# A bidirectional mLSTM and convolution layer on one core: its sweeps with whole fp32 products of the states, in an order laid down by a list schedule

## The chip, the cores and the metric

The kernel runs on one core of a Trainium2 chip. The metric is the device time of one execution in microseconds, smaller is better; times of several runs are given by their median.

## What is computed

One layer works on two sequences, a prompt of 1024 rows and a sample of 256 rows, each row 1024 numbers wide. They are handled as one sequence of 1280 rows, that is ten chunks of 128 rows (chunks 0 to 7 the prompt, 8 and 9 the sample). The reference, cut to what matters here:

```python
h = rms_norm(x, norm_g) * (1.0 + scale) + shift
cb, cc, cx, cz, q, k, v, o, mz, gpre, gmerge = split_combined(h @ w_in)
y_conv = cb * centred_dwconv3(cc * cx, conv_w, conv_b) * jax.nn.silu(cz)
# mlstm_chunkwise, one direction, per head (4 heads of 256), per chunk of 128 rows:
S   = einsum('td,sd->ts', qc, kc) * Dexp
num = einsum('ts,sd->td', S, vc) + inter_w * einsum('td,de->te', qc, C)
hm  = num / den
C   = decay * C + einsum('s,sd,se->de', w, kc, vc)        # the state, 256 x 256
# forward and backward results are added, normalised per head, and gated:
y_m = jax.nn.sigmoid(o) * hm * jax.nn.silu(mz)
merged = g_conv * (y_conv @ w_proj_conv) + g_mlstm * (y_m @ w_proj_mlstm)
out = rms_norm(x + gate * (merged @ w_out))
```

The state C passes from chunk to chunk, forward in one sweep and backward in the other. A chunk needs its incoming states of both directions before it can be finished. All results are float32.

## The kernel before

**Two ways to multiply.** Most products are made of split operands: a float32 tensor becomes a high part (a rounded copy of type fp32r, made on ScalarE) and a low part (the rest, made on GpSimd or VectorE), and TensorE adds three fp32r products, high by high, high by low and low by high. A product of operands of type float32 without a split is one instruction in the code; the trace shows it as two matmul records.

**The stages.** First come the modulation and the norm. Then `run` (L471) works through a list of products of the input projection (seven for each pair of column blocks, a Strassen scheme): one `product` (L330) is 24 matmuls of 320 columns, and beside it run the splits of the next weights and the work on earlier results. Generators can be stepped once per product: `weights` (L852) prepares exponentials, and `thirds` (L819) forms the gate row on VectorE out of eight blocks `wg`, each in two loads; per block it ends in a small matmul with `ones` (L823). Results that later stages need (q, k, v, the convolution branch `yc_dr`, the gates `og_dr` and `th_dr`) go to DRAM. k is stored twice: transposed in `kT_dr`, and by rows, already split, as `kn_drH` and `kn_drL`.

Up to L1054 (`hand.close()`) the instructions of each engine stand in the order in which the program calls them. From there on the framework's own scheduler orders them.

**The sweeps** (L1161 to L1379) go over four heads. `backward(h)` runs one sweep ahead and keeps its queries in `qcb`; `forward(h)` then finishes the chunks in pairs, while `backward(h + 1)` runs beside it. In a sweep, per chunk:

- `prep` (L1122) loads the two parts of k, weights v with `w` on ScalarE (`vH`) and forms the low part on VectorE (`vL`, L1129).
- `state` (L1143) makes 2 x 3 fp32r products of 258 columns into `pu` (L1150 to L1152), adds them to the decayed state C on VectorE (L1157; L1155 for a first chunk), and splits C with `split` (L1103): the high part on ScalarE (L1106), the low part on GpSimd (L1107).
- `query` (L1133) splits q in the same way, multiplies 2 x 3 times with the parts of C into `pq` (L1140), and copies the result out, scaled, on ScalarE (L1141).

`chunk_pair` (L1176) makes the scores q times k (L1192, plain float32), weighs them (L1196), forms the divisors `r` (L1199 to L1202), transposes the weighted scores (L1213), multiplies them with v (L1220, plain float32), and adds the two queries. `mlstm_out` (L1266) normalises five, three or two chunks together, transposes (L1282), gates with `og` (L1283), and stores `ym_dr`.

**The filler.** `zc_units` (L1317) is the product of the convolution branch with its projection: 32 units of 24 matmuls of 320 columns (L1312 to L1314), independent of the sweeps. Its inputs `y` come from `yc_dr` in two halves of the rows. `FILL` and `BACK` (L1344, L1345) say after which step of a sweep a unit is called.

**The end.** `merge` (L1395) multiplies one half of `ym_dr` with its projection (384 matmuls of 320 columns, into `accd`), and `finish` (L1408) makes the output projection (480 matmuls of 256 columns, L1422 to L1424), the residual and the last norm. The first half of the rows goes first.

All DMAs are issued from SyncE (SP in the profile), in one queue whose entries wait in turn.

Of the kernel before, what the change touches and what calls it, by code (L numbers as in the profile page):

```python
# [9 lines left out]
F32 = mybir.dt.float32  # L10
# [6 lines left out]
P = 128  # L17
# [22 lines left out]

@with_exitstack
def encoder_kernel(
# [35 lines left out]
    kn_dr = [dram.tile([T, D], F32, name="kn_dr" + part) for part in "HL"]  # L78
# [91 lines left out]
    def quarter(pool, nm):  # L170
        return tuple(pool.tile([P, 4, TH2], F32R, name=nm + part) for part in "HL")
# [152 lines left out]

    hstack = ctx.enter_context(ExitStack())
    hp = hstack.enter_context(tc.tile_pool(name="hp", bufs=1, side="right"))
    B = {(0, 0): quarter(hp, "b00"), (1, 0): quarter(hp, "b10"), (1, 1): quarter(hp, "b11")}


# [289 lines left out]
    def turn_one(p):  # L619
# [9 lines left out]
        def f():  # L629
            vt = [qtile() for _ in range(1 + key)]  # L630
            for (j0, jn), pv in zip(((0, 3), (3, 2)), pvs):
                js = slice(j0 * P, (j0 + jn) * P)
                if key:
                    A.copy(vt[0][:, js].bitcast(F32R), pv[:, :jn * P])
                    V.tensor_tensor(out=vt[1][:, js].bitcast(F32R), in0=pv[:, :jn * P], in1=vt[0][:, js],
                                    op=ALU.subtract)
                else:
                    A.copy(vt[0][:, js], pv[:, :jn * P])
            for dst, o in zip(kn_dr if key else (v_dr,), vt):
                store(dst[l * TH2:(l + 1) * TH2, r0:r0 + P].rearrange("(c p) d -> p c d", p=P),  # L640
                      o[:].rearrange("p (c d) -> p c d", d=P))
# [177 lines left out]
    def thirds(pool):  # L819

        def total(acc, n):
            pg = misc_tile()
            PE.matmul(pg[0:1, 0:2 * P], ones[:, 0:1], acc[:].rearrange("p s n -> p (s n)"), start=True, stop=True)  # L823
            yield
            V.tensor_scalar(out=acc[0:1].rearrange("p s n -> p (s n)"), in0=pg[0:1, 0:2 * P], scalar1=0.5, scalar2=None,
                            op0=ALU.mult)
            for s in range(2):
                store(gb_dr[s:s + 1, n * P:(n + 1) * P], acc[0:1, s])

        late = iter(())  # L830
        for n in range(KT):
            ns = slice(2 * D + n * P, 2 * D + (n + 1) * P)
            acc = pool.tile([P, 2, P], F32, tag="acc", bufs=2, name="gacc")
            G.memset(acc[:], 0.0)
            for s in range(2):
                dma(acc[0:1, s], b_ada[0:1, ns])
            for k in range(0, KT, 4):
                raw = pool.tile([P, 4, P], F32, tag="wg", bufs=1, name="wg")
                dma(raw[:], wada[:, k:k + 4, ns])
                next(late, None)  # L840
                yield
                next(late, None)
                yield
                for i in range(4):
                    for s in range(2):
                        V.scalar_tensor_tensor(out=acc[:, s], in0=raw[:, i], scalar=cols[:, 8 * s + k + i:8 * s + k + i + 1],
                                               in1=acc[:, s], op0=ALU.mult, op1=ALU.add)
            late = chain([None], total(acc, n))
        for _ in late:
            yield  # L850
# [196 lines left out]
    with tc.tile_pool(name="r2", bufs=5, side="right") as ring[0], \  # L1047
            tc.tile_pool(name="ab", bufs=1, side="right") as conv_pool[0]:
        run(ends[9])
        settle()  # L1050
    with tc.tile_pool(name="r4", bufs=8, side="right") as ring[0]:
        run(len(todo))
        settle()
    hand.close()  # L1054

# [7 lines left out]
    misc[0] = bstack.enter_context(tc.tile_pool(name="psB", bufs=3, space=PSUM))  # L1063
    psM = bstack.enter_context(tc.tile_pool(name="psM", bufs=1, space=PSUM))

    def acc_tile():
        return psM.tile([P, 512], F32, tag="acc", bufs=2, name="acc")

    yp = ctx.enter_context(tc.tile_pool(name="yp", bufs=8, side="right"))
# [3 lines left out]
    qcbs = [qkv.tile([P, NC - 2, HD + 2], F32, name=f"qcb{i}") for i in range(2)]  # L1073
    Cbuf = [qkv.tile([P, 2, HD + 2], F32, name=f"C{d}") for d in range(2)]
# [10 lines left out]
    def slot(c):  # L1085
        return c - (c > 7)

    def load_head(h, what):
        i, hs = h % 2, slice(h * HD, (h + 1) * HD)
        for t0, tn in ((640, 384), (0, 640), (1024, 256)):  # L1090
            ts_ = slice(t0, t0 + tn)
            cs = slice(t0 // P, (t0 + tn) // P)
            if "k" in what:
                dma(kTs[i][:, :, ts_], kT_dr[hs, ts_].rearrange("(b p) t -> p b t", p=P))
            if "v" in what:
                dma(vNs[i][:, cs, 0:HD], v_dr[ts_, hs].rearrange("(c p) d -> p c d", p=P))
            if "q" in what:
                dma(qTs[i][:, :, ts_], qT_dr[hs, ts_].rearrange("(b p) t -> p b t", p=P))
# [434 lines left out]
```

## Time and profile before

| | us |
|---|---|
| median of 3 runs (1824.59 to 1827.71) | 1827.34 |
| the profiled execution | 1823.46 |
| its span | 1821.7 |
| TensorE busy in it (93%) | 1693.2 |
| VectorE, ScalarE, GpSimd busy | 1030.8, 667.6, 831.4 |
| end of the input projection, last matmul of L337 | about 1232.8 |
| first matmul of `merge` | 1582.3 |
| last matmul | 1812.3 |

The span is what the trace covers; the profiled execution's time is 1.8 us longer. A matmul's busy time runs to the modelled end of its pipeline, 0.28 to 0.32 us, while the next one starts 0.12 to 0.15 us after it; so what a matmul costs in a dense row is the distance between two starts. "idle before" is the time in which an engine did nothing before an instruction, with what ended it. The prediction shows the lines that it rests on.

### The profile page before, as it was taken

How to read it: one execution, taken by the hardware profiler on the slowest of the kernel's cores; microseconds unless marked ns; L12 is line 12 of the kernel's file. 1: busy time of each engine (PE TensorE's matmuls, PEld its weight loads, DVE VectorE, ACT ScalarE, POOL GpSimd, SP SyncE). 2: the span in 40 equal slices, each digit the busy share in tenths (PEclk: the TensorE clock that was granted, in tenths of full speed). 3: DMA queues.
4: the chain of work that ended last, by engine and by line, in shares of the span. 5: the costliest groups of instructions: out<-in, count | busy, mean ns of one | idle time of the engine just before them, and what ended most of it. 6: DMA issues, size and time to landing. Idle time of an engine off the chain costs nothing.

```text
span 1821.7 us, 30022 instructions
## 1 busy us (share of the span) xinstructions
PE 1693.2 (93%) x11438; PEld 1630.9 (90%) x11438; DVE 1030.8 (57%) x1739; ACT 667.6 (37%) x1359; POOL 831.4 (46%) x661
## 2 busy tenths in 40 slices
PE   5789999999899999999999999996888788899997
PEld 1689999999788999999999999996877678799997
DVE  6874333277987554555555333332588777456645
ACT  6552333223434222222222223122576565434323
POOL 3443333234545466666665433333566364232422
PEclk9889999999999999999999999998999999999999
DMA  8223234223655222222221534349767865674631
GB/s 308 63 87 108 98 104 133 84 85 92 168 146 145 62 64 76 76 76 72 68 69 46 167 96 145 121 135 318 256 205 225 282 184 163 217 244 152 225 128 70
DMA packets 231427, 253.28 MB, mean 139 GB/s; under 512 B 13700, under 2 KB 190068, under 8 KB 230260
## 3 DMA queue, kind: packets, MB, share of 16 engines
q1 hardware_dynamic: 231284, 251.37, 43.7%
q8 instruction: 90, 1.47, 0.3%
q14 instruction: 53, 0.43, 0.1%
HBM read 177.85 MB, written 73.47 MB: 138 GB/s over the span
## 4 chain that ended last, share of the span: by engine, by line
PE 54%; DVE 6%; POOL 3%; issue 2%; DMA 2%; ACT 2%; SPq 0%; DVEq 0%; POOLq 0%; ACTq 0%
PE accx L337 35%; PE accd L1312 2%; PE accd L1313 2%; PE accd L1314 2%; PE accd L1423 2%; PE accd L1424 2%; PE accd L1422 2%; PE pq L1140 1%; POOL C1L L1107 1%; PE acc L1313 1%; PE acc L1312 1%; PE acc L1314 1%; POOL wl L161 1%; POOL C0L L1107 1%; PE misc L627 1%
## 5 line engine op out<-in xcount | busy, mean ns | idle before, releaser
L409 DVE TENSOR_TENSOR q<-accx,q 128x640 f32<-128x640 f32 x288 | 233.3, 820 | 420.2 <-PE accx L337 368.0
L161 POOL TENSOR_TENSOR wl<-comb,wh 128x512 fp32r<-128x512 f32 x176 | 236.3, 1344 | 488.3 <-ACT wh L160 403.3
L161 POOL TENSOR_TENSOR wl<-raw,wh 128x512 fp32r<-128x512 f32 x196 | 270.8, 1386 | 194.2 <-ACT wh L160 179.1
L337 PE MATMUL accx<-half,wh 128*128 128x320 f32 x1408 | 268.2, 313 | 5.4 <-ACT wh L160 5.4
L160 ACT CAST wh<-comb 128x512 fp32r<-128x512 f32 x176 | 108.6, 620 | 388.7 <-DVE comb L379 305.7
L337 PEld LDWEIGHTS accx<-half,wh 128*128 128x128 f32 x1408 | 223.5, 190 | 6.8 <-ACT wh L160 5.6
L160 ACT CAST wh<-raw 128x512 fp32r<-128x512 f32 (+1 forms) x212 | 136.2, 648 | 92.5 <-PE accd L1313 27.9
L337 PE MATMUL accx<-half,wl 128*128 128x320 f32 x704 | 162.2, 312 | 0.8 <-POOL wl L161 0.8
L498 ACT ACTIVATE q<-q,zero 128x640 f32<-128x640 f32 x80 | 66.4, 830 | 174.4 <-DVE q L409 155.3
L337 PEld LDWEIGHTS accx<-half,wl 128*128 128x128 f32 x704 | 119.0, 190 | 1.5 <-POOL wl L161 1.5
L1423 PE MATMUL accd<-wl,mH 128*128 128x256 f32 x320 | 90.2, 282 | 0.1
L1422 PE MATMUL accd<-wh,mH 128*128 128x256 f32 x320 | 90.1, 282 | 0.0
L1424 PE MATMUL accd<-wh,mL 128*128 128x256 f32 x320 | 90.0, 282 | 0.0
L337 PE MATMUL accx<-b10H,wh 128*128 128x320 f32 x352 | 82.4, 315 | 6.1 <-ACT q L934 5.9
L337 PE MATMUL accx<-t2H,wl 128*128 128x320 f32 x352 | 81.9, 314 | 4.2 <-POOL wl L161 4.1
L337 PE MATMUL accx<-b00H,wh 128*128 128x320 f32 x352 | 81.8, 314 | 2.4 <-DVE half L248 2.3
L337 PE MATMUL accx<-t2H,wh 128*128 128x320 f32 x352 | 82.4, 316 | 1.8 <-ACT wh L160 1.7
L1312 PE MATMUL acc<-y,wh 128*128 128x320 f32 x256 | 81.8, 323 | 0.7 <-ACT wh L160 0.3
L1313 PE MATMUL acc<-y,wh 128*128 128x320 f32 x256 | 81.2, 317 | 1.1 <-DMA y<-yc_drL 1.1
L337 PE MATMUL accx<-t3H,wh 128*128 128x320 f32 x352 | 80.6, 310 | 1.1 <-ACT wh L160 1.1
L1312 PE MATMUL accd<-y,wh 128*128 128x320 f32 x256 | 78.1, 313 | 3.5 <-DVE og L1283 3.5
L337 PE MATMUL accx<-b10H,wl 128*128 128x320 f32 x352 | 81.1, 312 | 0.2 <-POOL wl L161 0.2
(304 smaller groups left out, 4539.5 us busy)
## 6 DMA issues: line engine op xcount, KB each, us to landing
raw<-in_w_in_dram SPq DMA_DIRECT2D x96, 256.0 KB
raw<-in_w_in_dram SPq DMA_DIRECT2D x44, 512.0 KB
th_dr<-q SPq DMA_DIRECT2D x32, 320.0 KB
th<-th_dr SPq DMA_DIRECT2D x32, 320.0 KB
wa<-in_w_ada_dram SPq DMA_DIRECT2D x8, 1024.0 KB
raw<-in_w_proj_conv_dram SPq DMA_DIRECT2D x16, 512.0 KB
kH<-kn_drH SPq DMA_DIRECT2D x64, 128.0 KB
kL<-kn_drL SPq DMA_DIRECT2D x64, 128.0 KB
```

The costliest lines, as they stand in the source:

```text
L160: A.copy(wh[:], src)
L161: eng.tensor_tensor(out=wl[:], in0=src, in1=fp(wh[:]), op=ALU.subtract)
L337: PE.matmul(acc[:, q, 0:TQ], st_[:, k, :], m_[:, q * TQ:(q + 1) * TQ], start=k == 0 and n == 0, stop=k == 3 and n == 2)
L409: V.tensor_tensor(out=two(dst), in0=ps, in1=two(t), op=ALU.add)
L498: A.activation(out, in_, AF.Tanh, bias=zero[:, 0:1], scale=0.5)
L1107: leng.tensor_tensor(out=L[:], in0=src, in1=fp(H[:]), op=ALU.subtract)
L1312: PE.matmul(accs[q][:, :TQ], wh, yH, start=kt == 0, stop=False)
L1313: PE.matmul(accs[q][:, :TQ], wh, yL, start=False, stop=False)
L1314: PE.matmul(accs[q][:, :TQ], wl, yH, start=False, stop=kt == KT - 1)
L1422: PE.matmul(pd, sH, ws[0][:, k, :], start=kt == 0, stop=False)
L1423: PE.matmul(pd, sH, ws[1][:, k, :], start=False, stop=False)
L1424: PE.matmul(pd, sL, ws[0][:, k, :], start=False, stop=kt == KT - 1)
```

## The change

**Plain fp32 states.** A state's update is now 2 products of float32 operands, `k` by `wv`, and a query 2 products of `qT` by `C`, where each was 2 x 3 fp32r products. The splits of q, of C, of the weighted v and of k are gone; `kn_dr` is one tensor.

```diff
     def query(self, c, dst, tok):
...
+            def mm():
+                for kd in range(2):
+                    PE.matmul(pq[:, 0:HD + 2], qTs[i][:, kd, c * P:(c + 1) * P], C[:, kd, :], start=kd == 0, stop=kd == 1)
+
+            op("PE", .88, mm, r=[("qT", i, piece(c)), C], w=[pq])
...
     def state(self, c):
...
+            k, wv = buf(mp_, [P, HD], F32, "k", 6), buf(mp_, [P, HD + 2], F32, "wv", 4)
+            load(128, lambda: k[:], kn_dr[c * P:(c + 1) * P, h * HD:(h + 1) * HD], (), [k])
...
+            pu = buf(psM, [P, 2, 512], F32, "u", 1)
+
+            def mm():
+                for db in range(2):
+                    PE.matmul(pu[:, db, 0:HD + 2], k[:, db * P:(db + 1) * P], wv[:], start=True, stop=True)
```

**A list schedule.** The new class `Board` collects every operation of the sweeps and of the filler, with its engine, a cost in us (for a DMA its KB), what it reads and writes, and the buffers it takes. `order` plays them in time, always the one that can start first (within 0.25 us the one of the earlier step), and `play` calls them in the order found. `hand.close()` has moved behind it, so all engines and the SP queue stand in that order.

```diff
+    HANDOFF, EACH, ISSUE, LAND, KB_US = .2, .04, .4, 2.2, 230.0
+    SOON, AHEAD = .25, 1.5
...
+            t, o = min(((t, o) for t, o in can if o.eng == eng and t <= lim), key=lambda x: (x[1].low, x[1].step, x[0], x[1].n))
...
+    PACE = [min(4 + s, 12) if s < 10 else 12 + (s - 9) * 4 // 7 if s < 17 else 16 if s < 21 else min(17 + (s - 21) * 15 // 23, 32)
+            for s in range(10 * NH + 15)]
+    one, two_ = ([Sweep(h, (h < 2) ^ p, p) for h in range(NH)] for p in range(2))
```

Per head one sweep goes ahead of the other by ten steps; at each step one chunk of the ahead sweep of head h and one of the second sweep of head h - 1 are laid down, and `PACE` says how many filler units stand by then: all 32 by step 44 of 55. For heads 2 and 3 the second sweep runs backward, so the last rows done are those of the first half. Chunks are now normalised, transposed, gated and stored by pairs (`Pairs.finish`). `pu`, and `pq`, renamed `qc`, still have one buffer each.

**The filler's inputs.** They go where the operands `b00` and `b10` of the projection were, which its last five products no longer read, and are loaded with the first weights before those five:

```diff
+        loads.setdefault(len(todo) - 5, []).append(first_w)
+        loads.setdefault(len(todo) - 5, []).append(first_y)
+        run(len(todo) - 1)
+        ws_c.append([split_w(wp, r[:, :, 0:P], G) for r in raws_c])
+        run(len(todo))
+        ws_c.append([split_w(wp, r[:, :, P:2 * P], G) for r in raws_c])
```

**The end.** The second half of the rows is merged first. Its inputs are loaded and split inside the sweeps (`first_ym`, from step 45 on).

**`thirds`** is laid down as a plan. In step 4n + 4 VectorE still makes the second half of block n; its matmul moves from step 4n + 5 to 4n + 6, and the load of `wg` comes ahead of the memset of the sum and of the bias loads, which follow a step later:

```diff
+            for t, order, f in ((0, 3, (begin, n)), (0, 2, (load, n, 0)), (1, 0, (bias, n)), (2, 0, (use, n, 0)),
+                                (2, 1, (load, n, 1)), (4, 0, (use, n, 1)), (6, 1, (total, n)), (7, 0, (keep_row, n))):
```

**How the order moves.** First the SP queue, at the end of the input projection. The names: `raw` is a weight block of the convolution's projection, `y` the filler's input, `qT_dr` the last stores of the projection, `kT`, `vN`, `qT` a head's inputs. Before:

```order
L455 DMA qT_dr<-q 128x640
L1094 DMA kT_12155<-kT_dr 128x2x640
L1096 DMA vN_12156<-v_dr 128x5x256
L1098 DMA qT_12157<-qT_dr 128x2x640
L1094 DMA kT_12155<-kT_dr 128x2x256
L1096 DMA vN_12156<-v_dr 128x2x256
L1098 DMA qT_12157<-qT_dr 128x2x256
L1125 DMA kH<-kn_drH 128x256
L1125 DMA kL<-kn_drL 128x256
```

Now:

```order
L282 DMA raw<-in_w_proj_conv_dram 128x4x256 x2
L1193 DMA y<-yc_drH 128x4x640
L1193 DMA y<-yc_drL 128x4x640
L1193 DMA y<-yc_drH 128x4x640
L1193 DMA y<-yc_drL 128x4x640
L589 DMA v_dr<-q 128x5x128
L589 DMA qT_dr<-q 128x640 x4
L1235 DMA vN_12119<-v_dr 128x2x256
L1235 DMA raw<-in_w_proj_conv_dram 128x4x256 x2
L1235 DMA th<-th_dr 128x640
L1235 DMA k<-kn_dr 128x256
L1235 DMA qT_12120<-qT_dr 128x2x256
```

The filler's first inputs now stand ahead of the last five stores, and behind those the head's loads come in small pieces, `k` among them; on TensorE the first 48 matmuls behind the projection are the filler's, where before the scores of two chunks stood.

Second, GpSimd in the middle of the sweeps. The names: `C1L`, `C0L` and `qL` are low parts of the states and of q, `wl` those of the filler's weights. Before:

```order
L161 TENSOR_TENSOR wl<-raw,wh 128x512
L1107 TENSOR_TENSOR C1L<-C_12147,C1H 128x516
L1107 TENSOR_TENSOR C0L<-C_12146,C0H 128x516
L1107 TENSOR_TENSOR qL<-qT_12157,qH 128x256
L1107 TENSOR_TENSOR qL<-qT_12154,qH 128x256
L1107 TENSOR_TENSOR C1L<-C_12147,C1H 128x516
```

Now, from the sweeps' beginning (the memsets of the heads' `vN`) to their end, with the first splits of the merge behind them:

```order
L1228 MEMSET vN_12119 128x10
L1229 MEMSET vN_12119 128x10
L1228 MEMSET vN_12116 128x10
L1229 MEMSET vN_12116 128x10
L1483 TENSOR_TENSOR wl<-raw,wh 128x512 x28
L293 TENSOR_TENSOR wl<-raw,wh 128x512 x16
```

The 64 subtractions for q and the 64 for C are gone; the filler's 28 stand alone.

Third, TensorE at the end of the sweeps. The names: `misc<-kT,qT` are scores, `misc<-ident,Pt` and `misc<-vN,Ps` the transpose and the product with v, `misc<-ident,vN` (now `qcf`) the transposes ahead of the gate, `acc` the filler, `accd` the merge. Before:

```order
L1313 MATMUL acc<-y,wh 128x320
L1314 MATMUL acc<-y,wl 128x320
L1220 MATMUL misc<-vN_12153,Ps 128x256
L1282 MATMUL misc<-ident,vN_12153 128x128 x4
L1312 MATMUL accd<-y,wh 128x320
```

Now:

```order
L1338 MATMUL misc<-kT_12115,qT_12117 128x128 x2
L1375 MATMUL misc<-ident,Pt 128x128
L1378 MATMUL misc<-vN_12116,Ps 128x256
L1375 MATMUL misc<-ident,Pt 128x128
L1378 MATMUL misc<-vN_12116,Ps 128x256
L1425 MATMUL misc<-ident,qcf 128x128 x4
L1375 MATMUL misc<-ident,Pt 128x128
L1378 MATMUL misc<-vN_12116,Ps 128x256
L1425 MATMUL misc<-ident,qcf 128x128 x4
L1453 MATMUL accd<-b00H,wh 128x320
```

Before, filler stood between the last chunks' operations up to the last product with v. Now 33 rows stand between the last filler matmul and the merge, the last nine of them above: in all 5 queries, 4 updates, 5 scores, 7 transposes of scores, 7 products with v and 20 transposes, and nothing that is independent of the sweep.

More of the change, by code (lines that the diff above doesn't have):

```diff
@@ L831, in thirds @@
-        for n in range(KT):
[L832 to L848, printed above, removed]
@@ L1083, in encoder_kernel @@
         G.memset(vNs[i][:, :, HD + 1:HD + 2], 0.0)
[L1085 to L1098, printed above, removed]
```

726 lines of the change are left out of this document (461 added, 265 removed).

## The prediction

> **What bounds the kernel now.** I read the page first. TensorE (PE) is busy for 93% of the span; in the row of 40 slices it is full but for the start, a few slices, and slices 28 to 35, which are the sweeps.
>
> ```profile
> PE 1693.2 (93%) x11438; PEld 1630.9 (90%) x11438; DVE 1030.8 (57%) x1739; ACT 667.6 (37%) x1359; POOL 831.4 (46%) x661
> PE   5789999999899999999999999996888788899997
> ```
>
> Then the busy times by stretch. The first is the one with `thirds`, the second the rest of the input projection, the next five the sweeps, the last the end. Behind the times stand the granted clock, the DMA share and GB/s.
>
> ```profile
> core 0: us, PE busy (x) PEld busy (x) DVE busy (x) ACT busy (x) POOL busy (x), PEclk, DMA share, GB/s
> 429.00:575.00 146.00, 130.54 (x816) 122.06 (x815) 126.51 (x204) 57.12 (x127) 69.60 (x60) 0.96 0.56 150
> 575.00:1233.00 658.00, 655.71 (x4494) 654.25 (x4492) 311.69 (x373) 171.08 (x305) 350.62 (x255) 1.00 0.31 93
> 1233.00:1260.00 27.00, 11.81 (x58) 10.72 (x59) 4.61 (x8) 6.16 (x15) 6.86 (x7) 0.75 1.02 366
> 1260.00:1290.00 30.00, 29.76 (x214) 29.56 (x213) 10.79 (x21) 11.27 (x24) 15.06 (x14) 1.00 0.85 282
> 1290.00:1520.00 230.00, 193.72 (x1275) 171.87 (x1274) 177.85 (x444) 148.62 (x386) 133.03 (x122) 0.98 0.71 222
> 1520.00:1570.00 50.00, 47.16 (x326) 44.36 (x324) 32.51 (x105) 25.97 (x71) 19.84 (x17) 1.00 0.49 156
> 1570.00:1583.00 13.00, 5.64 (x34) 4.80 (x33) 6.60 (x15) 6.07 (x11) 3.27 (x2) 0.85 0.61 197
> 1583.00:1813.00 230.00, 228.69 (x1727) 227.72 (x1726) 131.68 (x227) 77.33 (x163) 72.00 (x67) 0.99 0.51 171
> ```
>
> The projection and the end are dense (1.3 us idle in the last 230). In the sweeps PE is idle for 15.2 + 0.2 + 36.3 + 2.8 + 7.4 = 62 us to be seen. Who ends it stands in the groups of the sweeps; the last two rows below are waits of the first stretch (total, times, longest):
>
> ```profile
> L1312 PE MATMUL acc<-y,wh 128*128 128x320 f32 x256 | 81.8, 323 | 0.7 <-ACT wh L160 0.3 <-DMA y<-yc_drH 0.2
> L1150 PE MATMUL pu<-vH,kH 128*128 128x258 f32 x128 | 39.1, 305 | 5.6 <-DVE C L1155 1.7 <-DVE C L1157 1.0 <-ACT qcf L1230 0.9
> L1192 PE MATMUL misc<-kT,qT 128*128 128x128 f32 x160 | 27.5, 295 | 11.5 <-DMA qT<-qT_dr 11.5
> L1220 PE MATMUL misc<-vN,Ps 128*128 128x256 f32 x80 | 26.0, 409 | 1.5 <-DVE og L1283 1.4
> L1282 PE MATMUL misc<-ident,vN 128*128 128x128 f32 x80 | 17.6, 298 | 10.2 <-ACT vN L1273 10.0
> L1140 PE MATMUL pq<-C1L,qH 128*128 128x258 f32 x64 | 16.3, 335 | 12.7 <-POOL C1L L1107 10.7 <-DMA vN<-v_dr 1.8
> L1213 PE MATMUL misc<-ident,Pt 128*128 128x128 f32 x40 | 11.8, 294 | 8.0 <-DVE Pt L1210 6.4 <-DVE rs_r L138 1.3
> L1107 POOL TENSOR_TENSOR qL<-qT,qH 128x256 fp32r<-128x256 f32 x64 | 50.5, 790 | 51.4 <-ACT qH L1106 41.9 <-PE acc L1314 5.5 <-PE misc L1213 2.8
> L1107 POOL TENSOR_TENSOR C1L<-C,C1H 128x516 fp32r<-128x516 f32 x32 | 43.0, 1343 | 38.0 <-ACT C1H L1106 33.4 <-PE misc L1213 1.8 <-DVE rs_r L138 1.8
> L1129 DVE SCALAR_TENSOR_TENSOR vL<-vN,gcol,vH 128x258 fp32r<-128x258 f32 x64 | 44.2, 693 | 6.6 <-ACT vH L1128 6.6
> PE misc L823 <- DVE gacc L846: 9.0, 7, 3.6
> DVE gacc L846 <- DMA wg<-in_w_ada_dram: 10.9, 9, 2.8
> ```
>
> So from one state to the next query lie an update on VectorE, a rounding on ScalarE and 1.34 us on GpSimd, and PE stands behind the last of them.
>
> **What a matmul costs.** Busy times overlap; I take distances between starts in dense rows of the timeline:
>
> ```profile
> 1539.83 0.28 PE L1150 MATMUL pu<-vH,kH 128*128 128x258 f32 x1
> 1540.54 0.31 PE L1312 MATMUL acc<-y,wh 128*128 128x320 f32 x1
> 1540.69 0.30 PE L1313 MATMUL acc<-y,wh 128*128 128x320 f32 x1
> ...
> 1563.66 0.61 PE L1192 MATMUL misc<-kT,qT 128*128 128x128 f32 x4
> 1564.10 0.60 PE L1220 MATMUL misc<-vN,Ps 128*128 128x256 f32 x2
> 1564.35 0.49 PE L1312 MATMUL acc<-y,wh 128*128 128x320 f32 x1
> 1564.68 0.31 PE L1313 MATMUL acc<-y,wh 128*128 128x320 f32 x1
> ```
>
> The six fp32r products of an update take 1540.54 - 1539.83 = 0.71 us, 0.118 each; one of 320 columns takes 0.147 (0.15 here). Two plain products of 128 columns (four records) take 0.44 us, so 0.11 a record; one of 256 columns takes 1564.68 - 1564.10 - 0.147 = 0.43. A plain product of 258 columns, which the trace lacks, is between that and 258/128 x 0.22 = 0.44; I take 0.44. A transpose of 128 columns is put at one record, 0.11.
>
> The sweeps' work before is 768 x 0.147 (filler) + 768 x 0.118 (states, queries) + 160 x 0.11 + 40 x 0.43 + 120 x 0.11 = 112.9 + 90.6 + 17.6 + 17.2 + 13.2 = 251.5 us. They last from the end of the projection to the merge:
>
> ```profile
> 1232.52 0.45 PE L337 MATMUL accx<-b11H,wl 128*128 128x320 f32 x2
> 1244.43 2.04 PE L1192 MATMUL misc<-kT,qT 128*128 128x128 f32 x8 [11.47 <-DMA qT<-qT_dr]
> ...
> 1573.52 0.59 PE L1220 MATMUL misc<-vN,Ps 128*128 128x256 f32 x2
> 1578.01 0.84 PE L1282 MATMUL misc<-ident,vN 128*128 128x128 f32 x4 [3.90 <-ACT vN L1273]
> 1582.32 0.63 PE L1312 MATMUL accd<-y,wh 128*128 128x320 f32 x1 [3.47 <-DVE og L1283]
> ```
>
> 1582.3 - 1232.8 = 349.5 us, so 98 us are lost, of which 62 are visible; 36 hide in pipelines that drain, 0.58 for each visible one.
>
> **The change part by part.**
>
> *Plain products: PE pays.* 64 updates and 64 queries of 2 products are 256 x 0.44 = 112.6 us in place of 90.6: 22 us more, and the sweeps' work becomes 273.5. The Trainium skill's page FP8 and Floating Point Precision (TensorE Precision Notes) speaks against this edit too: it counts four passes of the array for true fp32. By four passes at 0.118 a product would be 0.47, the work 8 us more, and the result 1791 in place of the 1783 below; the row with 0.43 is nearer, and I keep it.
>
> *What goes.* GpSimd loses 64 x 0.79 + 64 x 1.34 (both states) = 136 us of the 178 that it does in the sweeps, VectorE the 44.2 us of `vL`, ScalarE the roundings. All of it lay beside PE's work; what counts is that query and state no longer wait for it. VectorE's load in the sweeps was 232 us; without `vL` and with 8 more small norms it is about 200 in some 310, so it does not bound.
>
> *The start.* 11.5 us were lost waiting for `qT`, with a clock of 0.75 behind. Now the filler's 48 matmuls (7 us) stand first, and their inputs (5.2 MB, 14 us at the 366 GB/s of that stretch) are asked for five products of 24 x 0.147 us ahead, 17.6 us. What is late next: the loads of weights and of `k` behind them wait in SP's queue for the last splits of the projection. I allow 3 us; ends 0 and the 11.5 of today.
>
> *Inside.* With filler between the steps the stretch 1520 to 1570 loses 2.84 us visibly, with the hidden share 4.5 of 50, 9%; the stretch 1260 to 1290, nearly all filler, 1%; the stretch 1290 to 1520 loses 36.3 visibly, 57 of 230, 25%. The new order lays filler by the step, without GpSimd's waits; I take 8%, by the row 1520 to 1570. The work inside is 273.5 - 16 (the tail) - 7 (the start) = 250, so 20 us are lost; ends 3 (1%) and 83 (25%).
>
> *The tail.* Behind the last filler stand 9 x 0.88 (queries and updates) + 5 x 0.44 + 7 x 0.43 + 27 x 0.11 = 16 us of work. Before, from the last chunk's scores (1563.66) to its transposes (1578.01) it took 14.4 us; behind the last scores now stand 2.9 us of work, so 11.5 are lost, and I add 1.5 for the steps ahead. 13 us; ends 7 (the two gaps 3.9 + 3.5 of today) and 23 (two pairs waiting in full). The Trainium skill's page TensorE: Matmul & The Clock Gate (What's actually happening) has the clock at half after an idle window of about 3.4 us, and full again after as long a busy one. The rows agree (0.75 behind the first gap); by it such a tail makes the merge's start 1.7 us dearer and the result 1785.
>
> *The merge.* Its rows stay: 230 us. Today its inputs come through `og`, a store and a load; now those of the second half are split inside the sweeps, and those of the first half have the 57 us of the first output projection to arrive. No change, ends -2 and +4.
>
> *`thirds`.* PE no longer waits 9.0 us for VectorE, since the matmul comes a step (3.5 us) later and the longest wait is 3.6. But VectorE is busy for 126.5 of these 146 us, so it sets the pace; only its own waits for `wg`, 10.9 us, can shorten the stretch, and a load put ahead of a memset and two small loads cures a part. I take 4 us off; ends 0 and 14. The halved stores of k are off the path: nothing, covered by a projection that is 99.7% busy.
>
> *Sum.* Sweeps: 273.5 + 3 + 20 + 13 = 309.5, 40 less than 349.5. With `thirds` 44 us less. The profiled execution took 1823.5 (its span and 1.8 us), so 1779.5; it lies 3.9 us below the median, and I give the forecast against the median: 1827.3 - 44 = **1783**.
>
> **The rivals.**
>
> *Half the waits stay* (1804). The order is fixed by constants; where a real operation is late, all behind it on its engine are late, and `pu` and `qc` have one buffer each, so that an update waits until VectorE has read the one before. Inside is then lost 14%, halfway to the 25% of 1290 to 1520: 41 us in place of 20. For it speaks that PE's waits on VectorE and ScalarE (L1282 10.0, L1213 6.4) do not go with GpSimd's.
>
> *SP's queue holds k back* (1846, slower). `ym_dr` and `zc_dr` stores wait in the one queue for the end of long chains, and the loads of k, states and the filler's weights stand behind them. The chain of waits shows such loads at the end today:
>
> ```profile
> 1294.29 4.70 DMA vN<-v_dr
> 1373.94 2.34 DMA kH<-kn_drH
> ```
>
> If that keeps the loss inside at 25%, it is 83 us, 63 more than forecast, while PE pays its 22. It turns slower from 64 us of loss inside, 20%. There are 40 stores of `ym_dr` and 16 of `zc_dr`; each would have to cost PE 0.8 us beyond what six buffers of k cover. Against it: k's loads halve, and the DMA share falls with them.
>
> *More is won* (1758). The loss inside falls to 2% (5 us, 15 less), and `thirds` gives all of its 14.
>
> That the change doesn't do what it says I exclude: the order shows the splits gone and the filler ahead.
>
> **How the numbers follow.** Forecast 0.60, half the waits 0.20, more won 0.14, slower 0.06. The likeliest is 1783. The range holds the forecast, most of the middle rival and the better one: 1757 to 1816. About 0.2% (3.7 us) is what a measurement of this kernel tells from no change: faster 0.93, same 0.01, slower 0.06.
>
> **What would show it.** Right: a start of the merge near 1232.8 - 4 + 309.5 = 1538; distances of 0.88 us for two plain products; GpSimd busy for some 40 us in the sweeps; no gap over 3 us behind the projection; a gap of about 11 us ahead of the merge. Wrong: PE waiting inside for `k` or `qT` by DMA, or for `C` by VectorE, in sum over 64 us; or plain products at 0.47 and more.

## The result and the profile after

The changed kernel takes **1779.26 us** (median of 4 runs, 1778.43 to 1780.40), the kernel before 1826.05 beside it (4 runs, 1824.59 to 1827.71): a ratio of 0.9744, with a 95% interval from 0.9727 to 0.9761. The profiled execution took 1778.4 us, its span is 1776.7. The forecast was 1783.

The landmarks on TensorE first, from its timeline in the changed kernel. The columns are the start, how long, line, operation, tile and operands, shapes and count, and in brackets the idle time ahead and what ended it.

```profile
1229.02 0.45 PE L471 MATMUL accx<-b11H,wl 128*128 128x320 f32 x2
1230.43 0.38 PE L1522 MATMUL acc<-y,wh 128*128 128x320 f32 x1 [0.96 <-ACT wh L292]
1239.65 1.11 PE L1295 MATMUL u<-wv,k 128*128 128x258 f32 x4 [1.94 <-DMA th<-th_dr]
...
1442.00 1.03 PE L1295 MATMUL u<-wv,k 128*128 128x258 f32 x4
1442.87 1.03 PE L1277 MATMUL qc<-C,qT 128*128 128x258 f32 x4
1443.74 0.61 PE L1338 MATMUL misc<-kT,qT 128*128 128x128 f32 x4
...
1498.23 0.31 PE L1524 MATMUL acc<-b10H,wl 128*128 128x320 f32 x1
...
1512.69 1.14 PE L1277 MATMUL qc<-C,qT 128*128 128x258 f32 x4 [2.62 <-DVE C L1303]
...
1534.65 1.30 PE L1425 MATMUL misc<-ident,qcf 128*128 128x128 f32 x4 [3.33 <-ACT qcf L1418]
1536.53 0.64 PE L1453 MATMUL accd<-b00H,wh 128*128 128x320 f32 x1 [0.58 <-DVE og L1428]
```

The projection's last product starts at 1229.2 (the second of the first row), 3.5 us earlier than before. Two plain products (4 records) are 0.87 us apart, twice in a row. The last filler product is done at 1498.4, and the merge begins at 1536.5 (the stretch between them is called the tail below). So the sweeps last 1536.5 - 1229.3 = 307.2 us, 42.3 less than the 349.5 of before. With the forecast's work of 273.5 us, 33.7 are lost: 3 at the start (0.96 and 1.94), 38.1 - 16 = 22 behind the last filler, and 8.7 inside.

The table by stages shows the same. The columns are the stretch, its length, then the busy time of PE, PE's weight loads, VectorE, ScalarE and GpSimd with their counts, the granted clock, the DMA share and GB/s:

```profile
1290.00:1498.00 208.00, 204.77 (x1193) 186.34 (x1192) 134.96 (x470) 116.88 (x308) 25.73 (x20) 1.00 0.72 232
1498.00:1537.00 39.00, 23.07 (x103) 15.90 (x102) 30.74 (x95) 20.38 (x54) 3.08 (x2) 0.89 0.50 157
1537.00:1767.00 230.00, 229.91 (x1728) 229.70 (x1727) 129.08 (x220) 76.19 (x161) 72.29 (x67) 0.99 0.47 158
```

Inside, PE is busy for 98% of the time; in the tail for 23 of 39 us. The list of waits of PE over the whole sweeps (total, times, longest) adds up to 22.8 us, where 62 were seen before. It begins with these:

```profile
PE qc L1277 <- DVE C L1303: 7.5, 6, 2.6
PE misc L1425 <- ACT qcf L1418: 5.1, 3, 3.3
PE misc L1378 <- ACT Ps L1376: 2.9, 7, 0.8
```

Of the 7.5 us for the state C, 6.1 lie in the tail. The list names no wait for GpSimd and none for k; but the 1.94 us ahead of the first update stand under a load of `th`, which an update does not read, so another load may have been meant.

### The profile page after: what moved, and what is told of

Same layout as the page of the kernel before. It is cut to its first block, busy times and chain, and to the rows that moved or that the text cites. A ratio compares the mean times of both kernels' runs of the same rounds, so it can differ in the third digit from the quotient of the medians.

```text
span 1776.7 us, 29030 instructions
## 1 busy us (share of the span) xinstructions
PE 1687.2 (95%) x11182; PEld 1623.0 (91%) x11182; DVE 953.7 (54%) x1703; ACT 620.7 (35%) x1243; POOL 697.4 (39%) x533
## 4 chain that ended last, share of the span: by engine, by line
PE 63%; DVE 3%; issue 1%; ACT 1%; DMA 1%; POOL 0%; SPq 0%; ACTq 0%; DVEq 0%; POOLq 0%
PE accx L471 35%; PE qc L1277 3%; PE u L1295 3%; PE accd L1453 2%; PE accd L1454 2%; PE accd L1455 2%; PE accd L1667 2%; PE accd L1668 2%; PE accd L1666 2%; PE acc L1522 2%; PE acc L1523 2%; PE acc L1524 2%; PE misc L1378 1%; PE misc L1338 1%; DVE gacc L966 1%
## 5 line engine op out<-in xcount | busy, mean ns | idle before, releaser
L292 ACT CAST wh<-raw 128x512 fp32r<-128x512 f32 (+1 forms) x184 | 119.4, 654 | 72.5 <-PE accd L1668 20.3
L471 PE MATMUL accx<-t2H,wl 128*128 128x320 f32 x352 | 80.8, 311 | 5.4 <-POOL wl L293 5.4
L471 PE MATMUL accx<-b00H,wl 128*128 128x320 f32 x352 | 81.0, 311 | 1.1 <-POOL wl L293 1.1
L471 PE MATMUL accx<-t3H,wl 128*128 128x320 f32 x352 | 80.5, 310 | 1.2 <-POOL wl L293 1.1
```

The source lines that it names most:

```text
L292: A.copy(wh[:], src)
L471: PE.matmul(acc[:, q, 0:TQ], st_[:, k, :], m_[:, q * TQ:(q + 1) * TQ], start=k == 0 and n == 0, stop=k == 3 and n == 2)
```

## The experiments

The theory at first: the splits cost because TensorE stood behind a chain from an update over VectorE, ScalarE and GpSimd to the next query; the plain products and the planned order together take that away. The rivals: one of the two parts does it alone; and, after the first four runs, it is the load of the splits on VectorE and GpSimd and not the chain. Further runs take up the prediction's terms (the start, the tail, `thirds`).

### Split products in the new order

```
-    PE.matmul(pq[:, 0:HD + 2], qTs[i][:, kd, c * P:(c + 1) * P], C[:, kd, :], ...)
+    op("ACT", .45, lambda: A.copy(qH[:], src()), ...)
+    op("POOL", .79, lambda: G.tensor_tensor(out=qL[:], in0=src(), in1=fp(qH[:]), op=ALU.subtract), ...)
+    for n, (q, C) in enumerate(((qH, CH), (qL, CH), (qH, CL))): ...
+    op("ACT", .7, lambda: A.copy(CH[:], C1[:]), ...)
+    op("POOL", 1.34, lambda: G.tensor_tensor(out=CL[:], in0=C1[:], in1=fp(CH[:]), op=ALU.subtract), ...)
```

(and the same for k and wv, with k's halves from two arrays again; the halves of k and of wv have three buffers each in place of six and four, and the state is updated in place)

Expected: 

> The changed kernel, with the products of the states split into three fp32r products again, inside the list schedule (k's halves with three buffers each and the state updated in place, for want of room). Theory (the plain products pay because the chain from a state to the next query gets short): PE's work in the sweeps falls by 22 us, but GpSimd gets 64 x (0.79 + 1.34) = 136 us back and VectorE 44, and a chain of 0.7 + 1.34 us stands again between an update and its query; waits for C's low part and for wl come back and the start of the merge moves from 1536.5 to 1545 to 1580: 1785 to 1815 us. Rival A (the order alone does it, the plain products only cost): the 22 us are saved and little else changes, the merge starts at 1515 to 1525: 1757 to 1768 us.

Measured: 1808.14 us, ratio to the kernel before 0.992 (0.9898 to 0.9941). The merge begins at 1570.8. Both lie where the theory put them. The whole sweeps, in the split kernel:

```profile
1229.50:1570.80 341.30, 291.94 (x1897) 268.03 (x1896) 246.52 (x653) 202.98 (x518) 173.99 (x165) 0.93 0.72 230
```

and in the changed kernel:

```profile
1229.30:1536.50 307.20, 283.69 (x1642) 255.38 (x1640) 178.08 (x589) 152.19 (x390) 42.97 (x37) 0.99 0.71 230
```

Rival A falls: the order alone, with 22 us less work, is 34 us slower in the sweeps than with the plain products. But the theory's reason is not what the waits show. Of the 341.3 - 251.5 = 90 us lost, PE waits for GpSimd in 1.3 (15.5 in the kernel before, where the list schedule is missing):

```profile
PE misc L1452 <- ACT qcf L1445: 9.8, 8, 3.3
...
PE qc L1291 <- POOL C1L L1331: 0.7, 2, 0.4
PE qc L1291 <- POOL C0L L1331: 0.6, 1, 0.6
```

VectorE is busy for 246.5 us in place of 178.1. `wvL` explains 41.7 of these 68 us; the rest is the same operations taking longer. Groups of VectorE in the split kernel (busy, mean ns, idle ahead):

```profile
L1326 DVE SCALAR_TENSOR_TENSOR C<-C,decay,u 128x516 f32<-128x516 f32 x48 | 36.0, 749 | 26.7 <-PE u L1318 20.4 <-POOL C0L L1331 2.3 <-PE misc L1365 1.3
L1388 DVE TENSOR_TENSOR r<-r,den 128x4 f32<-128x4 f32 x20 | 15.0, 748 | 0.7
L1385 DVE SCALAR_TENSOR_TENSOR r<-den,gcol 128x4 f32<-128x4 f32 x20 | 9.4, 470 | 0.7
L1389 DVE RECIPROCAL r<-r 128x4 f32<-128x4 f32 x20 | 3.6, 178 | 0.7
```

and the same four in the changed kernel:

```profile
L1303 DVE SCALAR_TENSOR_TENSOR C<-C,decay,u 128x516 f32<-128x516 f32 x48 | 36.0, 750 | 30.8 <-PE u L1295 30.3
L1362 DVE RECIPROCAL r<-r 128x4 f32<-128x4 f32 x20 | 3.6, 178 | 0.7
L1358 DVE SCALAR_TENSOR_TENSOR r<-den,gcol 128x4 f32<-128x4 f32 x20 | 3.4, 170 | 0.6
L1361 DVE TENSOR_TENSOR r<-r,den 128x4 f32<-128x4 f32 x20 | 3.2, 162 | 0.7
```

An operation on 4 columns with two inputs in SBUF takes 748 ns in place of 162; the reciprocal (one input) and the update of the state (its second input is in PSUM) are as before. This gave the second theory, tried below.

### Plain products in the old order

```
-    qH, qL = split(mp_, self.qT[:, :, tsl], "q", [P, 2, P], leng=G)
-    CH, CL = self.parts
-    for n, (q, C) in enumerate(((qH, CH), (qL, CH), (qH, CL))):
-        for kd in range(2):
-            PE.matmul(pq[:, 0:HD + 2], q[:, kd, :], C[:, kd, :], start=n + kd == 0, stop=n + kd == 3)
+    for kd in range(2):
+        PE.matmul(pq[:, 0:HD + 2], self.qT[:, kd, tsl], Cbuf[self.d][:, kd, :], start=kd == 0, stop=kd == 1)
```

(and the same for the updates; k is kept and loaded once)

Expected: 

> The kernel before, with plain fp32 products of the states and no splits, all else as it was. Theory (both parts are needed): 22 us more work, and of the waits PE loses those on GpSimd (10.7 + 4.5 + 0.3 us seen, with what hides behind them 25) and some on ScalarE and VectorE; the wait for qT, for vN and at the end stay. 1810 to 1830 us, a draw. Rival B (the plain products alone give most of the gain, and the order is decoration): 1790 us or less.

Measured: 1791.04 us, ratio 0.9826 (0.9806 to 0.9846). The theory's draw is a miss, and rival B's bound of 1790 is missed by a microsecond: 31 of the 47 us come with the plain products alone. The old start is still there, and so is the old end:

```profile
1242.66 2.04 PE L1174 MATMUL misc<-kT,qT 128*128 128x128 f32 x8 [11.13 <-DMA qT<-qT_dr]
...
1549.37 0.64 PE L1294 MATMUL accd<-y,wh 128*128 128x320 f32 x1 [3.91 <-DVE og L1265]
```

The projection ended at 1231.4, so the sweeps last 318.0 us. With the run above, both parts and each alone (length of the sweeps; us lost behind the work of 251.5 or 273.5):

| | split products | plain products |
|---|---|---|
| old order | 349.5; 98 lost | 318.0; 44.5 lost |
| list schedule | 341.3; 90 lost | 307.2; 33.7 lost |

The plain products save 54 to 56 us of loss for 22 us of work, in either order. The order saves 8 to 11, with either products. The two hardly depend on each other.

### The operations as they stand in the source

```
-        for o in sorted(self.order(), key=lambda o: (o.start, o.n)):
+        for o in self.ops:
```

Expected: 

> The changed kernel with its sweeps' operations issued as they stand in the source, step after step, instead of in the order of the list schedule. Theory (the loss inside is small because the schedule asks for loads ahead of the stores that wait, and puts filler where an operation would be late): the loads of k, of weights and of th then stand behind stores that wait for finished rows; 36 such stores at 1 to 3 us each, PE waits for k or th by DMA over 30 us in sum: 1810 to 1860 us, the rival of the prediction in which SP's queue holds k back. Rival C (steps with filler between them are enough, the list schedule adds little): 1779 to 1790 us, PE's waits by DMA under 8 us.

Measured: 2191.24 us, ratio 1.2025 (1.2 to 1.205), so 412 us more. The sweeps last 716 us; PE's longest waits, and the stage's row with its clock (0.74, the sixth figure behind the length):

```profile
PE u L1295 <- DMA k<-kn_dr: 80.8, 26, 7.4
PE misc L1425 <- ACT qcf L1418: 67.7, 20, 4.9
```

```profile
1229.30:1945.40 716.10, 425.91 (x1642) 330.66 (x1641) 177.03 (x585) 145.39 (x386) 41.73 (x37) 0.74 0.29 96
```

Rival C falls. The slower rival of the prediction (k held back in SP's queue) is a real mechanism, 80.8 us, and the list schedule is what keeps it away. But the larger part is another: in the source a consumer stands right behind its producer, and PE waits for VectorE and ScalarE at every step, 193 us in the whole list, and its products take 426 us of busy time at that clock in place of 284. The expectation had the mechanism, but 31 to 81 of the 412 us. So "the order is worth 10 us" holds against the old hand-made order, not against none.

### `thirds` in its old order

```
-   (0, 3, (begin, n)), (0, 2, (load, n, 0)), (1, 0, (bias, n)), ... (6, 1, (total, n)), (7, 0, (keep_row, n))
+   (0, 1, (begin, n)), (0, 2, (bias, n)), (0, 3, (load, n, 0)), ... (5, 1, (total, n)), (6, 2, (keep_row, n))
```

Expected: 

> The changed kernel with the gates' thirds in their old order: the sum's matmul one step earlier, the result kept one step earlier, the memset and the bias ahead of the load. Theory (that edit is worth the 3.5 us by which the projection ended earlier): 1782 to 1784 us, PE waiting for gacc by 6 to 9 us again and the projection's end at 1232 to 1233. Rival D (the 3.5 us came from the stores of k that were halved or from the rest of the order): 1778 to 1780 us, and the projection's end stays at 1229.

Measured: 1781.86 us, ratio 0.9777 (0.9757 to 0.9797); its interval overlaps that of the changed kernel, 0.9727 to 0.9761. PE's wait for the sum is back (8.6 us, 6 times, as before: 9.0). Between the same two products of the projection (30% and 50% of its 7392) lie 244.8 us here, 242.8 in the changed kernel and 246.3 before. So the edit is worth 2.0 of the 3.5 us of that stretch; in the other runs of the changed kernel with this part as it is, the stretch takes 242.4 to 243.6. The remaining 1.5 us are not placed. They are not the halved stores of k: the run with plain products in the old order stores k once too, and takes 246.4. The time, 1781.86, lies a little below the theory's 1782 to 1784. The projection's end, 1229.7, is rival D's and not the theory's, but it does not tell much: it lies anywhere from 1227.3 to 1229.6 in runs that are alike up to there.

### GpSimd's load beside

```
+   op("POOL", .79, lambda: G.tensor_tensor(out=s1_[:], in0=qTs[i][:, :, qs_], in1=qTs[i][:, :, qs_], op=ALU.subtract), ...)
+   op("POOL", 1.34, lambda: G.tensor_tensor(out=s2_[:], in0=src_(), in1=src_(), op=ALU.subtract), ...)
```

Expected: 

> The changed kernel with 128 more GpSimd subtractions into places that nobody reads: 64 of 256 columns beside the queries and 64 of 512 beside the updates, the size of the splits that the change removed. The rest of the work is whole. Theory 1 (the chain: the splits cost because PE stood behind them): nothing waits for these, so 1778 to 1782 us. Theory 2 (the load: GpSimd's splits stretch VectorE's small operations, as in the run with the split in the new order, where r<-r,den took 748 ns on average in place of 162): VectorE's busy time in the sweeps goes from 178 to 205 us or more, and part of the 34 us of that run comes back, 3 to 12: 1782 to 1791 us.

Measured: 1794.25 us, ratio 0.9838 (0.982 to 0.9856): 15 us more by the medians, 17 by the ratios, for work whose results nobody reads. TensorE's order is nearly the same (18 of the 3369 matmul records behind the projection stand elsewhere), and no wait of PE or VectorE in the sweeps is put down to GpSimd. The sweeps and the group that grows most (14.5 us, 373 ns each in the changed kernel):

```profile
1229.30:1553.00 323.70, 292.13 (x1638) 259.37 (x1636) 201.88 (x588) 150.96 (x389) 144.76 (x165) 0.96 0.67 217
```

```profile
L1380 DVE SCALAR_TENSOR_TENSOR Pt<-abc,r,Pt 128x128 f32<-128x128 f32 x40 | 22.1, 564 | 0.2
```

Theory 1 falls as the whole story. VectorE's busy time is 24 us up with the same instructions, and the waits of PE behind it grow, among them those for `qcf` from 5.1 to 8.2 us and for `Ps` from 2.9 to 5.3.

### GpSimd's and VectorE's load beside

```
+   op("DVE", .69, lambda: V.scalar_tensor_tensor(out=s3_[:], in0=vNs[i][:, c, :], scalar=gcol[:, 3, self.d, h, c:c + 1],
+                                                 in1=vNs[i][:, c, :], op0=ALU.mult, op1=ALU.subtract), ...)
```

Expected: 

> The same with 64 more operations of 0.69 us on VectorE as well, whose results nobody reads: the load of the three fp32r products without anybody waiting for it. Theory 1 (the chain): 1778 to 1785 us. Theory 2 (the load): VectorE's busy time in the sweeps goes to some 246 us as with the split, it is busy for over 50 of the 60 us from 1350 to 1410, and most of the loss comes back: 1795 to 1812 us.

Measured: 1801.88 us, ratio 0.9883 (0.9865 to 0.9901): 23 us more by the medians, 25 by the ratios.

```profile
1229.30:1565.20 335.90, 298.33 (x1642) 262.64 (x1641) 245.10 (x653) 152.16 (x390) 150.25 (x165) 0.95 0.65 211
```

VectorE is busy for 245 us, as with the split, and the sweeps are 335.9 - 307.2 = 29 us longer in this execution. The split lost 56 us more than the plain products in the same order; so the load of VectorE and GpSimd, with nobody waiting for its results, makes about half of that. About, because GpSimd is busy for 150 us here and for 174 with the split, and because the list schedule counts the added operations and moves TensorE's order more than in the run before (245 of 3369 records). The other half is the chain itself, ScalarE's roundings (203 us busy in place of 152) and the fewer buffers of k of that run, and is not told apart.

### The filler's inputs late

```
-        loads.setdefault(len(todo) - 5, []).append(first_w)
-        loads.setdefault(len(todo) - 5, []).append(first_y)
-        run(len(todo) - 1)
         run(len(todo))
         settle()
+        first_w()
+        first_y()
```

(the two splits of the weights follow)

Expected: 

> The changed kernel with the filler's first weights and products asked for and split when the projection is done, not five products ahead. Theory (the early inputs are what the new order is worth at the start, 11.5 us of waiting before, some 3 now): PE waits 8 to 14 us behind the projection, 1787 to 1793 us. Rival E (the order inside and at the end is what the schedule gives, 10.8 us over the plain products in the old order, and the start is worth little): 1779 to 1783 us.

Measured: 1797.28 us, ratio 0.9854 (0.984 to 0.9868), 18 us more. PE's timeline:

```profile
1239.88 0.60 PE L1521 MATMUL acc<-y,wh 128*128 128x320 f32 x1 [10.45 <-DMA y<-yc_drH]
1243.11 0.64 PE L1522 MATMUL acc<-y,wh 128*128 128x320 f32 x1 [2.62 <-DMA y<-yc_drL]
1249.77 0.42 PE L1522 MATMUL acc<-y,wh 128*128 128x320 f32 x1 [2.80 <-DMA y<-yc_drL]
```

15.9 us of waiting where 2.9 stood. Rival E falls. It is dearer than the expected 8 to 14, and dearer than the 11.5 of before: filler at the head of the order, without its inputs, is worse than the old start. The early loads into finished operands' places belong to the order: without them it is 6 us behind the plain products in the old order (1791.04), though the intervals of the two just overlap.

### The tail's subtractions on GpSimd

```
-   op("DVE", .9, lambda raw=raw, k=k: V.tensor_tensor(out=y[1][:, k], in0=raw[:], in1=fp(y[0][:, k]), ...
+   op("POOL", 1.7, lambda raw=raw, k=k: G.tensor_tensor(out=y[1][:, k], in0=raw[:], in1=fp(y[0][:, k]), ...
```

Expected: 

> The changed kernel with the low parts of the second half's finished rows (8 subtractions of 128x640, 0.82 us and more each) on GpSimd in place of VectorE, behind the last filler. Theory (VectorE, busy for 30.7 of these 39 us, sets the tail's pace, and the subtractions stand ahead of updates in its order): the tail shrinks from 38 to 30 to 35 us, 1771 to 1776 us. Rival F (the tail is the chain's own latency, VectorE's load is beside it, and GpSimd beside VectorE stretches it): 1778 to 1782 us.

Measured: 1778.21 us, ratio 0.975 (0.9736 to 0.9764), no difference. The first 37 us of the tail, in the changed kernel and in this run:

```profile
1498.00:1535.00 37.00, 21.64 (x98) 14.92 (x96) 29.83 (x93) 20.38 (x54) 3.08 (x2) 0.91 0.50 160
1498.00:1535.00 37.00, 21.91 (x96) 15.82 (x95) 26.10 (x85) 19.67 (x54) 14.82 (x10) 0.87 0.50 156
```

The merge begins at 1536.9 (1536.5). VectorE has less to do, and the tail is as long. So VectorE's load does not set it, and rival F's time stands. That it is the chain of small steps between four engines is argued here, and put to the test below by laying work between them.

### The filler spread further

```
-  ... else min(17 + (s - 21) * 15 // 23, 32)
+  ... else min(17 + (s - 21) * 15 // 28, 32)
-        if s == 45:
+        if s == 50:
             ym0 = [first_ym(0)]
```

Expected: 

> The changed kernel with the filler's second half spread over 28 steps in place of 23, so that its last product stands ahead of the last 2 of 40 values in TensorE's order (7 before), and the finished rows of the second half are asked for 5 steps later. Theory (since the split on GpSimd did not shorten the tail, the tail is a chain of short steps between four engines, and filler put between them is done for nothing): up to 12 of the tail's 22 lost us go, the merge starts at 1522 to 1530: 1764 to 1772 us. Rival G (the places of the finished rows come free later, and the loads, copies and 8 subtractions behind them give it back at the merge's start): PE waits 5 us and more for b00 and b10, 1776 to 1785 us.

Measured: 1771.26 us, ratio 0.9705 (0.9689 to 0.9721), which lies below the changed kernel's 0.9727 to 0.9761. The merge begins at 1532.8, later than the 1522 to 1530 expected, and no wait for b00 or b10 stands ahead of it, so rival G falls. What is left are two turns of a pair's own chain, one behind the other:

```profile
1518.47 0.30 PE L1524 MATMUL acc<-b10H,wl 128*128 128x320 f32 x1
...
1524.48 1.31 PE L1425 MATMUL misc<-ident,qcf 128*128 128x128 f32 x4 [3.57 <-ACT qcf L1418]
...
1530.95 1.30 PE L1425 MATMUL misc<-ident,qcf 128*128 128x128 f32 x4 [3.37 <-ACT qcf L1418]
```

### The filler to the end

```
+  ... else min(17 + (s - 21) * 15 // 32, 32)
+        if s == 54:
             ym0 = [first_ym(0)]
```

(and the low parts on GpSimd)

Expected: 

> The same over 32 steps, with the low parts on GpSimd: the filler's last product stands behind all but one pair of transposes, and the finished rows are asked for at the last step. Theory: the tail's waits go, but now the 8 copies of 0.8 us and the subtractions, which wait for the filler's last product, stand alone ahead of the merge: 1770 to 1780 us, no better than with 28 steps, PE waiting 5 to 12 us for b00. Rival H (the loads, copies and subtractions hide behind the last steps): 1760 to 1768 us.

Measured: **1769.68 us**, ratio 0.9695 (0.968 to 0.9709), the lowest median of all, though not clear of the run before it (0.9689 to 0.9721). The merge begins at 1525.2, 11 us earlier than in the changed kernel, but waits 4.1 us in its first products for the copies, the low parts and `og`:

```profile
PE accd L1453 <- ACT b00H L1543: 1.2, 1, 1.2
PE accd L1454 <- POOL b00L L1544: 1.1, 2, 0.8
PE accd L1453 <- DVE og L1428: 1.0, 1, 1.0
PE accd L1454 <- POOL b10L L1544: 0.8, 3, 0.4
```

Rival H's time is missed by 1.7 us and the theory's by 0.3, but the wait is shorter than the 5 to 12 us of the theory: a part of the copies and subtractions does hide.

### The filler to the end, the finished rows early

```
-            raw = buf(thp, [P, TH2], F32, "th", 3)
+            raw = buf(thp, [P, TH2], F32, "ymr", 3)
```

(with `s == 45` and VectorE's subtractions as in the changed kernel)

Expected: 

> The run with filler to the end, with three places of their own for the finished rows that are loaded ahead of the merge (they shared three with the filler's th), the rows asked for at step 45 again, and the low parts on VectorE, which stood idle there. Theory (in that run the merge began at 1525.2 but then waited 4.1 us for copies and low parts, behind loads that came late): the merge begins at 1523 to 1526 and waits under 2 us: 1764 to 1768 us, the fastest of all. Rival J (the copies wait for the filler's last product whatever the loads do, and ScalarE's eight copies of 0.73 us set the pace): 1768 to 1772 us, as with filler to the end.

Measured: 1770.94 us, ratio 0.9708 (0.9694 to 0.9722). The merge waits for no copy any more, but begins at 1529.0. VectorE's timeline ahead of it:

```profile
1524.91 2.86 DVE L1544 TENSOR_TENSOR b00L<-ymr,b00H 128x640 fp32r<-128x640 f32 x3 [1.59 <-ACT b00H L1543]
...
1528.09 0.86 DVE L1428 SCALAR_TENSOR_TENSOR og<-misc,mhq,og 128x256 f32<-128x256 f32 x2
```

The rows came early, so three copies and three subtractions now stand ahead of the last `qcf` and `og`, for which PE waits. The wait changed its place, not its size. The time is rival J's, by another way; the theory falls.

### The bias by another queue

```
-                dma(accs[n][0:1, s], b_ada[0:1, 2 * D + n * P:2 * D + (n + 1) * P])
+                A.dma_start(accs[n][0:1, s], b_ada[0:1, 2 * D + n * P:2 * D + (n + 1) * P])
```

Expected: 

> The changed kernel with the 16 small loads of the gates' bias issued by ScalarE in place of SyncE. Theory (in the changed order VectorE waits 12.4 us for that bias, which stands in SP's queue behind loads that wait for their places, and VectorE, busy for 121 of the 146 us from 429 to 575, sets that stretch's pace): VectorE's wait for the bias goes, and the stretch is 4 to 8 us shorter: 1771 to 1776 us. Rival I (another wait stands right behind, for wg or the weights' low parts on GpSimd, 7.5 us): 1777 to 1781 us.

Measured: 1782.27 us, ratio 0.9766 (0.975 to 0.9782), no gain; between the same two products of the projection as above lie 244.9 us, 2 more than in the changed kernel. VectorE waits 4.5 us for `wg` (2.8 in the changed kernel) in the stretch 429 to 575, and still for the bias (12.4 us, 4 times, there):

```profile
DVE gacc L966 <- DMA gacc<-in_b_ada_dram: 11.3, 6, 3.4
```

Out of SP's queue the bias comes as late as in it: ScalarE issues its loads at 443.2 and 497.5 us, where SyncE did at 444.2 and 498.8. So the theory falls. The time is a microsecond above rival I's, but its reason (another wait right behind) is not what the list shows: the wait for the bias itself stays, and what holds it is open.

## Why the prediction was right, and where it was not

- **Plain products at 0.44 us:** 0.435 by distances of 0.87 us for two. The Trainium skill's page FP8 and Floating Point Precision (TensorE Precision Notes) counts four passes of the array for true fp32. At the price of an fp32r product each they would be 0.47, the prediction's estimate, and that price is not what the rows show; how many passes there are, they do not tell.
- **The start, 3 us:** 2.9. Shown by undoing it: 15.9 us.
- **Inside, 20 us:** 8.7. The size is wrong: the 8%, taken from the row 1520 to 1570 of before, was too much. That row still had the splits in it. With the plain products alone, in the old order, the stretch 1290 to 1487 shows 6.7 us of idle PE in 197, where the stretch 1290 to 1520 of before showed 36.3 in 230; in the changed kernel it is 3.2 in 208.
- **The tail, 13 us:** 22, near the upper end. Behind the last scores (they start at 1522.2) 11.4 us are lost, where 11.5 were forecast, in several gaps of at most 3.3 us. The fit is in part luck, since the row of before that gave the 11.5 ends at the transposes, ahead of a last gap of 3.5 us. What was mis-sized are the 1.5 us for the steps ahead of them: 10.7 are lost there. Queries, updates, scores and values stand there with nothing between them, each with its own gap, and 6.1 us of these gaps are queries waiting for the state from VectorE. Inside and tail together were put at 33 us and are 31: the merge's start (1538 forecast, 1536.5 measured) came out right by luck, from two wrong terms.
- **The merge, 230 us unchanged:** 230.5. Its first products are dear, see below, but they were so before.
- **`thirds`, 4 us:** the stretch gave 3.5, of which the edit is worth 2.0; PE's 9.0 us of waiting went as said, but its waits for weights grew from 6.4 to 11.8 us, while VectorE waited 12.4 us for the bias. What of this hangs on the other the runs do not tell.
- **"What counts is that query and state no longer wait for it":** this step failed as the main reason. In the kernel before, PE did wait 15.5 us for GpSimd; but with the split in the new order it waits 1.3 us and still loses 90. The step that put VectorE's load without `vL` at about 200 us took its other operations at their old prices; it is 178, since GpSimd no longer stretches them. About half of the splits' cost in the new order is that load; the other half is not told apart. No number of the sum hung on it, so the forecast stood.
- **The rivals:** half the waits did not stay (33.7 us lost in all). The slower one was averted by the list schedule, not impossible. Inside, the loss came near the 5 us of the better rival, but the tail took 9 us more than forecast.

## What to carry to other kernels

Work that nobody waits for can set the time of the engines beside it: before a split is priced by its chain, price what its subtractions on GpSimd do to VectorE's operations, group by group, at the two means. Test a change of two parts as a table of four, since a gain that looks like scheduling may come for three quarters (31.5 of the sweeps' 42.3 us here) from the arithmetic. And the tail behind the last filler was not shortened here by unloading its busiest engine; filler laid into it gave 8 to 10 us, up to the point at which what is waiting for the filler's places becomes the tail.

## What the runs showed of the hardware

**GpSimd stretches some of VectorE's operations.** In the split kernel, VectorE's timeline and GpSimd's in the same place:

```profile
1360.56 0.76 DVE L1385 SCALAR_TENSOR_TENSOR r<-den,gcol 128x4 f32<-128x4 f32 x1
1361.35 0.65 DVE L1388 TENSOR_TENSOR r<-r,den 128x4 f32<-128x4 f32 x1
```

```profile
1360.02 1.28 POOL L1331 TENSOR_TENSOR C0L<-C,C0H 128x516 fp32r<-128x516 f32 x1
1361.25 0.74 POOL L1284 TENSOR_TENSOR qL<-qT,qH 128x256 fp32r<-128x256 f32 x1
```

The first ends at 1361.32, GpSimd's first at 1361.30; the second at 1362.00, GpSimd's second at 1361.99. An operation of 0.17 us ends when GpSimd's does. The Trainium skill's page SBUF — State Buffer (SBUF: two separate sides) says that VectorE and GpSimd share a pair of ports, held by one for a whole instruction, and that of VectorE's operations those with two inputs in SBUF need it against a reading GpSimd, and those in a mode that takes both ports. The groups above agree: those with two inputs in SBUF are stretched, the update and the reciprocal are not. Two more groups are stretched that have a single input (`rs_t<-rs_t` from 225 to 431 ns, `ssqm<-ssqm` from 163 to 268); whether they run in such a mode the trace does not show. And one with two inputs (`rstm<-rs_t,rs_r`) stays at 160 ns in the split kernel, but takes 285 beside GpSimd's added load.

**A tail full of gaps leaves a slow clock behind.** The merge's first products in the changed kernel:

```profile
1536.96 0.47 PE L1454 MATMUL accd<-b00L,wh 128*128 128x320 f32 x1
1537.23 0.47 PE L1455 MATMUL accd<-b00H,wl 128*128 128x320 f32 x1
...
1541.96 0.31 PE L1455 MATMUL accd<-b10H,wl 128*128 128x320 f32 x1
1542.10 0.30 PE L1453 MATMUL accd<-b10H,wh 128*128 128x320 f32 x1
```

They are 0.27 us apart at first and 0.14 to 0.15 from 1541.96 on: 5 us, some 19 products, 2.3 us dearer. The prediction's estimate was 1.7. But the kernel before pays for this too, behind its two gaps of 3.9 and 3.5 us (0.27 apart until 1585.95, 3.6 us behind the merge's start), so the merge as a whole is only 0.5 us longer. With the filler laid to the end they are 0.15 apart from the second on. In the source order, with gaps at every step, the granted clock was 0.74, and PE was busy for 426 us with the products that took 284.
